# A two-layer hybrid trunk: gate rows kept as rows in a DRAM table and fetched by DMA, and a rotary step with one temporary

## The chip, the cores and the metric

One Trainium2 chip, one core. The metric is the device time of one execution in microseconds; an execution that is profiled gives a span (first to last instruction of the program) and its own device time beside it. The engines are TensorE (PE for matmuls, PEld for weight loads), VectorE (DVE), ScalarE (ACT), GpSimd (POOL) and SyncE (SP), which issues DMA transfers.

## The reference, cut to what matters

A trunk of two layers over 256 latent and 256 context tokens of width 1024, all in float32. Each layer is a half-step SwiGLU block, a mixing block (gated MLP over chunks, differential attention, windowed attention, joined by one output projection) and a second half-step SwiGLU block. Each block is modulated by nine vectors that come from a conditioning vector:

```python
def adaln_in(s, g_pre, shift, scale):
    return rmsnorm(s, g_pre) * (1 + scale) + shift

def adaln_out(s, y, g_post, gate, weight):
    return s + weight * gate * rmsnorm(y, g_post)

mod_x = (silu(c) @ w_mod[l] + b_mod[l]).reshape(b_, 9, 1, 1024)      # for latent tokens
mod_h = (silu(c_ctx) @ w_mod[l] + b_mod[l]).reshape(9, 1, 1024)      # for context tokens
# vectors 3j, 3j+1, 3j+2 are shift, scale and gate of block j (0: first FFN, 1: mixing, 2: second FFN)
# weight is 1/2 for the FFNs and 1 for the mixing

rot = jnp.concatenate([-x2, x1, -x4, x3], axis=-1)                   # quarters of a head
return x * cos + rot * sin                                           # apply_rope, latent q and k alone
```

In the last layer the context tokens take part only as keys and values.

## The kernel before, in words

Activations lie feature-major in Yh and Yl (128 partitions, 8 blocks of features, 512 tokens): a float32 number is split in a high part in the matmul's rounded format (hi, Yh, Uh) and the rest (lo, Yl, Ul), and a product is three matmuls, hi by hi, hi by lo and lo by hi (acc3, acc3_multi). Weights come in chunks of up to 1 MB into one of three staging buffers (tag stg), all issued by SyncE, and are split by ScalarE (L231) and VectorE or GpSimd (L100) into one of three pairs hi and lo.

A feed-forward block runs over pairs of 128-wide blocks of the 2816 hidden features, in three phases (6, 8 and 8 blocks); hidden() makes tanh, products and the split of a hidden block, in buffers of the tag p (six of them, function half). After each phase down() projects back. In the last phase the result of a token block is multiplied by the gate rows gp (L496), scaled by its norm and added to the stream S in residual(), and turn_y() normalises, transposes and modulates it for the next block. The mixing block makes keys, queries and values (L673 to L695 apply the rotary step to the latent ones), and then softmax units, spatial gating, normalisations and transposes are interleaved with the remaining projections.

The interleaving is by a model clock: every matmul helper calls tick() with its columns, and generators that are due (softmax units, turn_y, halves of the modulation) emit their next piece there; drain(tag) runs a kind of piece to its end. The order that the program text has is then used as priority by the framework's planner, which may move an instruction ahead in its engine's queue when its operands and its buffer allow it: a load of the second layer's mixing parameters (dl, L630) is issued at 544.61 us, in the middle of the first mixing. Buffers of one tag are reused in turn, and every queue, SyncE's and GpSimd's too, is in order.

The modulation is made by halves (mod_half, 512 of one vector's 1024 values): VectorE sums the eight 128-row slices of the weights, times the conditioning, into two accumulators of 128 partitions (L343, L345); four matmuls with ones add the partitions and spread each sum over 32 partitions (L350); ScalarE copies it (L355); two transposes turn it feature-major (L359), and mod_put adds the bias, multiplies by the norm's gain and writes coef (L322 to L331). 32 halves run so, two weight chunks each, about one in a step of the feed-forward loops; twelve of them are gates (q % 3 == 2). The first eight blocks' shift and scale come from mod_first.

gate_rows(l, j, st) makes two tiles gp of 128 x 512 in which every partition holds the gate row of a block for one kind of tokens: it is called once for each kind of tokens, twice in each of three feed-forward blocks and in the first mixing, once in the last mixing and in the last block: ten calls, each of 2 x 4 matmuls of a broadcast coefficient column with the identity (L401) and two ScalarE copies (L405).

## Time and profile before

| what | value |
|---|---|
| time, median of 3 runs | 1799.17 us (1795.40 to 1800.07) |
| the profiled execution: time, span | 1797.35 us, 1795.6 us |
| granted TensorE clock, mean over the span | 0.995 |
| busy: PE, PEld | 1749.6 us (97%), 1472.5 us (82%) |
| busy: DVE, ACT, POOL | 1188.4 us (66%), 709.9 us (40%), 161.1 us (9%) |
| moved by DMA | 250.79 MB, mean 140 GB/s |
| chain that ended last | PE 85%, DVE 7%, ACT 3%, POOL 2%, issue 2%, DMA 1% |

Busy time is the union of an engine's instructions. Matmuls are pipelined: a record of a 512-column matmul is about 0.37 to 0.39 us long, while the next one starts 0.23 us later, so the price of a matmul on its queue is read from the distance of starts. A small TensorE operation is listed twice where the float32 operand takes two passes.

### The profile page before, as it was taken

How to read it: one execution, taken by the hardware profiler on the slowest of the kernel's cores; microseconds unless marked ns; L12 is line 12 of the kernel's file. 1: busy time of each engine (PE TensorE's matmuls, PEld its weight loads, DVE VectorE, ACT ScalarE, POOL GpSimd, SP SyncE). 2: the span in 40 equal slices, each digit the busy share in tenths (PEclk: the TensorE clock that was granted, in tenths of full speed). 3: DMA queues.
4: the chain of work that ended last, by engine and by line, in shares of the span. 5: the costliest groups of instructions: out<-in, count | busy, mean ns of one | idle time of the engine just before them, and what ended most of it. 6: DMA issues, size and time to landing. Idle time of an engine off the chain costs nothing.

```text
span 1795.6 us, 24957 instructions
## 1 busy us (share of the span) xinstructions
PE 1749.6 (97%) x9847; PEld 1472.5 (82%) x9847; DVE 1188.4 (66%) x2195; ACT 709.9 (40%) x1520; POOL 161.1 (9%) x149
## 2 busy tenths in 40 slices
PE   6999999999999999999999999999999999999998
PEld 4788888889877689888787898787788897689997
DVE  4866876875467567668866476778764655765654
ACT  3323313244376653233222343332233535755443
POOL 3000000022312120000000120000000331010000
PEclk9999999999999999999999999999999999999999
DMA  9545554533120134465554233655544133226552
GB/s 327 192 135 182 188 188 141 164 124 106 59 95 27 35 96 153 138 202 165 180 171 141 70 100 121 203 169 195 174 142 141 46 96 118 71 89 194 188 188 71
DMA packets 190002, 250.79 MB, mean 140 GB/s; under 512 B 4666, under 2 KB 127804, under 8 KB 189884
## 3 DMA queue, kind: packets, MB, share of 16 engines
q1 hardware_dynamic: 189884, 249.19, 42.7%
q8 instruction: 77, 1.26, 0.3%
q14 instruction: 41, 0.34, 0.1%
HBM read 248.12 MB, written 1.05 MB: 139 GB/s over the span
## 4 chain that ended last, share of the span: by engine, by line
PE 85%; DVE 7%; ACT 3%; POOL 2%; issue 2%; DMA 1%; POOLq 0%; DVEq 0%; ACTq 0%
PE pa L241 26%; PE pa L245 13%; PE pb L254 6%; PE pb L260 6%; PE pb L262 6%; PE pa L254 5%; PE pa L262 5%; PE pa L260 5%; PE pb L241 3%; DVE lo L100 2%; PE pb L245 1%; PE pa L1208 1%; PE pc L350 1%; PE pa L770 1%; PE pc L791 1%
## 5 line engine op out<-in xcount | busy, mean ns | idle before, releaser
L100 DVE TENSOR_TENSOR lo<-stg,hi 128x512 fp32r<-128x512 f32 (+2 forms) x468 | 365.3, 820 | 189.9 <-ACT hi L231 114.3
L231 ACT ACTIVATE hi<-stg 128x512 fp32r<-128x512 f32 (+3 forms) x508 | 325.2, 701 | 321.1 <-PE pa L254 106.3
L241 PE MATMUL pa<-Yh,hi 128*128 128x512 f32 (+1 forms) x1168 | 417.2, 366 | 0.0
L241 PE MATMUL pa<-Yl,hi 128*128 128x512 f32 (+1 forms) x1168 | 414.4, 364 | 0.0
L345 DVE SCALAR_TENSOR_TENSOR acc<-stg,sT,acc 128x512 f32<-128x512 f32 x448 | 306.8, 746 | 4.3 <-DMA stg<-in_w_mod_dram 4.3
L245 PE MATMUL pa<-Yh,lo 128*128 128x512 f32 (+1 forms) x1168 | 258.6, 363 | 0.0
L241 PEld LDWEIGHTS pa<-Yh,hi 128*128 128x128 f32 x1168 | 220.4, 189 | 40.9 <-issue 7.8
L241 PEld LDWEIGHTS pa<-Yl,hi 128*128 128x128 f32 x1168 | 220.5, 189 | 34.5 <-issue 1.2
L245 PEld LDWEIGHTS pa<-Yh,lo 128*128 128x128 f32 x1168 | 202.2, 189 | 35.3 <-DVE lo L100 0.3
L543 ACT ACTIVATE Uh<-ha 128x512 fp32r<-128x512 f32 (+1 forms) x92 | 50.6, 551 | 278.7 <-DVE ha L541 278.7
L254 PE MATMUL pb<-hi,Ul 128*128 128x512 f32 x400 | 157.1, 393 | 0.0
L260 PE MATMUL pb<-hi,Uh 128*128 128x512 f32 x400 | 156.9, 393 | 0.0
L262 PE MATMUL pb<-lo,Uh 128*128 128x512 f32 x400 | 156.0, 390 | 0.0
L496 POOL TENSOR_TENSOR Z<-Z,gp 128x512 f32<-128x512 f32 x14 | 20.0, 1430 | 1179.5 <-ACT pb L495 1179.5
L541 DVE TENSOR_TENSOR ha<-ha,pa 128x512 f32<-128x512 f32 (+1 forms) x91 | 53.3, 585 | 82.5 <-PE pa L245 81.7
L260 PE MATMUL pa<-Yh,hi 128*128 128x256 f32 x368 | 92.0, 285 | 0.0
L262 PE MATMUL pa<-Yl,hi 128*128 128x256 f32 x368 | 91.3, 283 | 0.0
L539 ACT ACTIVATE ht<-pa 128x512 f32<-128x512 f32 (+1 forms) x91 | 46.5, 511 | 111.6 <-PE pa L245 82.8
L254 PEld LDWEIGHTS pb<-hi,Ul 128*128 128x128 f32 x400 | 75.1, 188 | 16.6 <-issue 1.2
L262 PEld LDWEIGHTS pb<-lo,Uh 128*128 128x128 f32 x400 | 75.1, 188 | 15.7 <-DVE lo L100 0.4
L260 PEld LDWEIGHTS pb<-hi,Uh 128*128 128x128 f32 x400 | 75.2, 188 | 15.5 <-issue 0.4
L100 POOL TENSOR_TENSOR lo<-stg,hi 128x512 fp32r<-128x512 f32 (+3 forms) x44 | 70.0, 1597 | 179.5 <-ACT hi L231 167.6
(290 smaller groups left out, 2772.1 us busy)
## 6 DMA issues: line engine op xcount, KB each, us to landing
stg<-in_w_mod_dram SPq DMA_DIRECT2D x64, 1024.0 KB, 5.1
stg<-in_ffn_w_gate_dram SPq DMA_DIRECT2D x43, 1024.0 KB, 5.4
stg<-in_ffn_w_up_dram SPq DMA_DIRECT2D x43, 1024.0 KB, 5.3
stg<-in_ffn_w_down_dram SPq DMA_DIRECT2D x32, 1024.0 KB, 5.0
stg<-in_w_in_dram SPq DMA_DIRECT2D x14, 1024.0 KB, 5.2
stg<-in_ffn_w_down_dram SPq DMA_DIRECT2D x16, 768.0 KB, 4.5
mst<-in_w_mod_dram SPq DMA_DIRECT2D x8, 1024.0 KB, 9.2
stg<-in_w_out_dram SPq DMA_DIRECT2D x8, 1024.0 KB, 6.2
```

What stands on the lines that cost most here:

```text
L100: eng.tensor_tensor(lo, full, f32(hi), op=ALU.subtract)
L231: nc.scalar.activation(hi[:, a:b, :], v[:, a:b, :], AF.Copy)
L241: nc.tensor.matmul(o, lhsT=ah, rhs=r, start=(i == 0), stop=(i == n - 1))
L245: nc.tensor.matmul(o, lhsT=al, rhs=bh, start=(i == 0), stop=(i == n - 1))
L254: nc.tensor.matmul(o, lhsT=al, rhs=bh, start=False, stop=last, skip_group_check=True)
L260: nc.tensor.matmul(o, lhsT=ah, rhs=bh, start=(first and k == 0), stop=False, skip_group_check=True)
L262: nc.tensor.matmul(o, lhsT=ah, rhs=bl, start=False, stop=False, skip_group_check=True)
L345: nc.vector.scalar_tensor_tensor(a, v[:, k, :], sc, a, op0=ALU.mult, op1=ALU.add)
L496: (nc.vector if hf else nc.gpsimd).tensor_tensor(zv, zv, gp[hf], op=ALU.mult)
L539: nc.scalar.activation(t, g, AF.Tanh, scale=0.5)
L541: nc.vector.tensor_tensor(a, a, u, op=ALU.mult)
L543: nc.scalar.activation(uh, a, AF.Copy)
```

## The change

The gate vectors no longer go through coef. A gate half keeps its sums as rows: the bias and the gain of the norm are loaded by SyncE, spread over the same 32-partition groups (by_groups, four transfers of 32 partitions x 256 values each), VectorE adds and multiplies in that layout, and GpSimd issues four stores of one partition's 256 values into a small table in DRAM (gtab). gate_rows becomes two fetches by SyncE, each of 512 values of a table row into all 128 partitions; in down() and in the first mixing it is called after the weights of the first half have been requested. norm_post is no longer in the parameter columns par. The transposes and mod_put of the other halves are put in a list (flips) which is emptied behind the next half's matmuls or when a modulation tag is drained. In the rotary step ScalarE writes the destination itself, which is then shuffled into the one temporary, multiplied in place by GpSimd and added to by VectorE.

```diff
@@ -75,6 +75,7 @@
     psc = ctx.enter_context(tc.tile_pool(name="psc", bufs=2, space=PSUM))
+    dr = ctx.enter_context(tc.tile_pool(name="dr", bufs=1, space=bass.MemoryType.DRAM))
     cnt = [0]
@@ -130,9 +131,17 @@
+    flips = []
+    def flip_now():
+        while flips:
+            flips.pop(0)()
     def drain(tag):
...
             run_next()
+        if tag[0] == "m":
+            flip_now()
@@ -152,7 +161,9 @@
     Yl = big.tile([P, KB, NT], F32R, name="Yl")
-    coef = const.tile([P, DEPTH, 9, KB, 2], F32, name="coef")
+    coef = const.tile([P, DEPTH, 3, 2, KB, 2], F32, name="coef")
+    gtab = {(l, j): dr.tile([2, D], F32, name=f"gate{l}{j}") for l in range(DEPTH) for j in range(3)}
@@ -162,17 +173,15 @@
     nc.sync.dma_start(rows[16:64, :], norm_pre.rearrange("l j (r p) -> (l j r) p", p=P))
-    nc.sync.dma_start(rows[64:112, :], norm_post.rearrange("l j (r p) -> (l j r) p", p=P))
-    nc.sync.dma_start(rows[112:114, :], diff_subln)
+    nc.sync.dma_start(rows[64:66, :], diff_subln)
     load_in(cx[0], 2)
-    par = const.tile([P, 114], F32, name="par")
+    par = const.tile([P, 66], F32, name="par")
     pt = pc()
-    nc.tensor.transpose(pt[:, 0:114], rows[0:114, :], ident[0:114, 0:114])
-    nc.vector.tensor_copy(par, pt[:, 0:114])
-    nc.vector.tensor_scalar(par[:, 16:112], par[:, 16:112], math.sqrt(D), None, op0=ALU.mult)
+    nc.tensor.transpose(pt[:, 0:66], rows[0:66, :], ident[0:66, 0:66])
+    nc.vector.tensor_copy(par, pt[:, 0:66])
+    nc.vector.tensor_scalar(par[:, 16:64], par[:, 16:64], math.sqrt(D), None, op0=ALU.mult)
     npre = par[:, 16:64].rearrange("p (l j b) -> p l j b", l=DEPTH, j=3)
-    npost = par[:, 64:112].rearrange("p (l j b) -> p l j b", l=DEPTH, j=3)
@@ -311,8 +320,8 @@
     def mod_put(l, q, b, n, src, mid):
-        dst = coef[:, l, q, b:b + n, :]
         j, kind = q // 3, q % 3
+        dst = coef[:, l, j, kind, b:b + n, :]
@@ -322,13 +331,16 @@
         nc.vector.tensor_tensor(mid, src, bias, op=ALU.add)
-        if kind == 1:
-            nc.vector.scalar_tensor_tensor(dst, mid, 1.0, bc(npre[:, l, j, b:b + n]),
-                                           op0=ALU.add, op1=ALU.mult)
-        else:
-            nc.vector.scalar_tensor_tensor(dst, mid, 1.0 if j == 1 else 0.5,
-                                           bc(npost[:, l, j, b:b + n]), op0=ALU.mult,
-                                           op1=ALU.mult)
+        nc.vector.scalar_tensor_tensor(dst, mid, 1.0, bc(npre[:, l, j, b:b + n]),
+                                       op0=ALU.add, op1=ALU.mult)
+    def by_groups(src):
+        r = wk.tile([P, 256], F32, tag="sq", name=nm("gr"), bufs=7)
+        for j in range(4):
+            nc.sync.dma_start(r[32 * j:32 * j + 32, :],
+                              src[256 * (j % 2):256 * (j % 2) + 256].partition_broadcast(32))
+        return r
@@ -344,24 +356,43 @@
                                                        op1=ALU.add)
+        gate = q % 3 == 2
+        j = q // 3
+        if gate:
+            br = by_groups(b_mod[l, c0:c0 + 512])
+            gr = by_groups(norm_post[l, j, hf * 512:(hf + 1) * 512])
         yield T_MOD
         t = pc()
-        for j in range(4):
-            nc.tensor.matmul(t[32 * j:32 * j + 32, 0:256], lhsT=ones[:, 0:32],
-                             rhs=acc[j // 2][:, 256 * (j % 2):256 * (j % 2) + 256],
-                             start=True, stop=True, tile_position=(0, 32 * j))
+        for i in range(4):
+            nc.tensor.matmul(t[32 * i:32 * i + 32, 0:256], lhsT=ones[:, 0:32],
+                             rhs=acc[i // 2][:, 256 * (i % 2):256 * (i % 2) + 256],
+                             start=True, stop=True, tile_position=(0, 32 * i))
         tick(1024)
+        flip_now()
+        if gate:
+            w = math.sqrt(D) * (1.0 if j == 1 else 0.5)
+            nc.vector.tensor_tensor(br, t[:, 0:256], br, op=ALU.add)
+            nc.vector.scalar_tensor_tensor(br, br, w, gr, op0=ALU.mult, op1=ALU.mult)
+            for i in range(4):
+                f0 = hf * 512 + 256 * (i % 2)
+                nc.gpsimd.dma_start(gtab[l, j][i // 2:i // 2 + 1, f0:f0 + 256],
+                                    br[32 * i:32 * i + 1, :])
+            return
         ev = wk.tile([P, 256], F32, tag="sq", name=nm("modev"), bufs=7)
         nc.scalar.activation(ev, t[:, 0:256], AF.Copy)
-        yield T_FLIP
-        u = pc()
-        for i in range(2):
-            nc.tensor.transpose(u[:, i * P:(i + 1) * P], ev[:, i * P:(i + 1) * P], ident)
-        tick(600)
-        uv = u[:, 0:256].rearrange("p (i s h r) -> p h i s r", i=2, s=2, h=2)
-        tmp = sm.tile([P, 2, 2, 2], F32, tag="modt", name=nm("modt"))
-        for h in range(2):
-            mod_put(l, q, 4 * hf + 2 * h, 2, uv[:, h, :, :, 0], tmp[:, h])
+        def turn():
+            u = pc()
+            for i in range(2):
+                nc.tensor.transpose(u[:, i * P:(i + 1) * P], ev[:, i * P:(i + 1) * P], ident)
+            tick(600)
+            uv = u[:, 0:256].rearrange("p (i s h r) -> p h i s r", i=2, s=2, h=2)
+            tmp = sm.tile([P, 2, 2, 2], F32, tag="modt", name=nm("modt"))
+            for h in range(2):
+                mod_put(l, q, 4 * hf + 2 * h, 2, uv[:, h, :, :, 0], tmp[:, h])
+        flips.append(turn)
@@ -396,13 +427,7 @@
         for hf in range(2):
-            t = pc()
-            for i in range(4):
-                nc.tensor.matmul(t[:, i * P:(i + 1) * P],
-                                 lhsT=coef[:, l, 3 * j + 2, 4 * hf + i, st:st + 1].to_broadcast([P, P]),
-                                 rhs=ident, start=True, stop=True)
-            tick(1600)
-            nc.scalar.activation(gp[hf], t, AF.Copy)
+            nc.sync.dma_start(gp[hf], gtab[l, j][st, hf * 512:(hf + 1) * 512].partition_broadcast(P))
         return gp
@@ -439,8 +464,8 @@
                     nc.scalar.activation(f[:, i * n:(i + 1) * n], t[:, i * n:(i + 1) * n], AF.Identity,
-                                         scale=coef[:, l, 3 * j + 1, b0 + i, st:st + 1],
-                                         bias=coef[:, l, 3 * j, b0 + i, st:st + 1])
+                                         scale=coef[:, l, j, 1, b0 + i, st:st + 1],
+                                         bias=coef[:, l, j, 0, b0 + i, st:st + 1])
                 fv = f.rearrange("p (b q) -> p b q", b=nb)
@@ -485,7 +510,7 @@
             st = sidx(s)
-            gp = gate_rows(l, j, st)
+            gp = []
             ss = {tb: sm.tile([P, 2], F32, tag="ss", name=nm("ss")) for tb in own}
@@ -509,6 +534,8 @@
                     ws[hf] = [chunk(hf, 0), chunk(hf, 1, into)]
+                if not hf:
+                    gp[:] = gate_rows(l, j, st)
                 for tb in own:
@@ -638,7 +665,7 @@
         gs = const.tile([P, 1], F32, name=nm("gsub"))
-        nc.vector.tensor_scalar(gs, par[:, 112 + l:113 + l], 1.0 - lam_init, None, op0=ALU.mult)
+        nc.vector.tensor_scalar(gs, par[:, 64 + l:65 + l], 1.0 - lam_init, None, op0=ALU.mult)
         sk = const.tile([P, 4], F32, name=nm("sink"))
@@ -670,14 +697,14 @@
         def rope_evac(dst, ps, scale):
-            scr = wk.tile([P, 256], F32, tag="t256", name=nm("scr"))
-            nc.scalar.activation(scr, ps, AF.Copy, scale=scale)
+            nc.scalar.activation(dst, ps, AF.Copy, scale=scale)
             sh = wk.tile([P, 256], F32, tag="t256", name=nm("shf"))
-            nc.vector.stream_shuffle(sh, scr, shmask)
-            nc.gpsimd.tensor_tensor(scr, scr, ropet[:, 0, :], op=ALU.mult)
+            nc.vector.stream_shuffle(sh, dst, shmask)
             nc.vector.tensor_tensor(sh, sh, ropet[:, 1, :], op=ALU.mult)
-            nc.vector.tensor_tensor(dst, sh, scr, op=ALU.add)
+            nc.gpsimd.tensor_tensor(dst, dst, ropet[:, 0, :], op=ALU.mult)
+            nc.vector.tensor_tensor(dst, dst, sh, op=ALU.add)
@@ -1114,7 +1141,7 @@
             st = sidx(s)
-            gp = gate_rows(l, 1, st)
+            gp = []
             bank = pb if s == HS else pa
@@ -1131,6 +1158,8 @@
                     ws[1][1] = chunk(1, 1)
+                if hf == hfs[0]:
+                    gp[:] = gate_rows(l, 1, st)
                 for tb in tbs[s]:
@@ -1175,7 +1204,7 @@
                     t = XT[:, b, s[0]:s[1]]
-                    nc.vector.tensor_scalar(t, t, coef[:, 0, 1, b, i:i + 1], coef[:, 0, 0, b, i:i + 1],
+                    nc.vector.tensor_scalar(t, t, coef[:, 0, 0, 1, b, i:i + 1], coef[:, 0, 0, 0, b, i:i + 1],
                                             op0=ALU.mult, op1=ALU.add)
...
                     nc.scalar.activation(yh, t, AF.Copy)
```

## Rows read from the trace of the kernel before

**Rows 1.** Sums by stage: start:end, length; PE, PEld, DVE, ACT, POOL busy; clock; DMA.
```profile
60.00:425.00 365.00, 365.00 (x1730) 295.88 (x1729) 272.63 (x458) 123.07 (x223) 17.30 (x15) 1.00 0.50 162
...
452.00:685.00 233.00, 220.45 (x1448) 185.95 (x1447) 150.33 (x358) 132.29 (x375) 51.76 (x42) 0.99 0.22 74
685.00:1435.00 750.00, 749.32 (x3797) 623.59 (x3797) 511.11 (x863) 244.82 (x453) 33.32 (x31) 1.00 0.45 146
1435.00:1605.00 170.00, 158.98 (x1099) 137.59 (x1098) 109.31 (x238) 93.71 (x237) 33.19 (x30) 0.99 0.29 94
1605.00:1795.60 190.60, 183.38 (x1288) 172.32 (x1286) 107.28 (x181) 85.30 (x161) 4.31 (x4) 0.98 0.48 155
```

**Rows 2.** Groups by line, whole span: shapes xcount | busy us, mean ns | idle before.
```profile
L401 PE MATMUL pc<-ident,coef 128*128 128x128 f32 x160 | 20.0, 275 | 0.8 <-ACT CU L797 0.8
L359 PE MATMUL pc<-ident,modev 128*128 128x128 f32 x64 | 12.2, 271 | 0.0
L880 DVE TENSOR_TENSOR gq<-gq,gx 128x256 f32<-128x256 f32 x12 | 5.1, 423 | 0.2
L324 DVE TENSOR_TENSOR modt<-pc,bm 128x4 f32<-128x4 f32 x44 | 5.0, 154 | 3.0 <-PE pc L359 3.0
```

**Rows 3.** Timeline of weight loads before the first block's last projection: start us, us.
```profile
362.05 0.37 PEld L359 LDWEIGHTS pc<-ident,modev 128*128 128x128 f32 x2
362.39 0.19 PEld L241 LDWEIGHTS pa<-Yh,hi 128*128 128x128 f32 x1
...
365.05 1.98 PEld L401 LDWEIGHTS pc<-ident,coef 128*128 128x128 f32 x16
366.94 0.19 PEld L260 LDWEIGHTS pb<-hi,Uh 128*128 128x128 f32 x1
```

**Rows 4.** Timeline of matmuls of two calls of gate_rows in the first mixing.
```profile
588.30 1.16 PE L401 MATMUL pc<-ident,coef 128*128 128x128 f32 x8 [0.79 <-ACT CU L797]
...
639.89 1.95 PE L401 MATMUL pc<-ident,coef 128*128 128x128 f32 x16
```

**Rows 5.** DMA issues by line: xcount, KB each, median us from issue to landing.
```profile
stg<-in_w_mod_dram SPq DMA_DIRECT2D x64, 1024.0 KB, 5.1
...
bs<-in_gmlp_b_s_dram SPq DMA_DIRECT2D x8, 32.0 KB, 3.3
```

**Rows 6.** Timeline of SyncE's queue: start us, us, xcount issues in a row.
```profile
53.70 1.83 SPq L650 DMA_DIRECT2D bs<-in_gmlp_b_s_dram  x3
```

**Rows 7.** Waits, whole span: who waited for whom: us in total, times, longest us.
```profile
SPq L203 <- DVE lo L100: 1018.6, 138, 44.7
...
ACT hi L231 <- PE pa L254: 106.3, 16, 12.7
...
ACT hi L231 <- PE pa L241: 80.2, 39, 3.1
```

**Rows 8.** Timeline of TensorE: the matmuls of two gate halves of the first block.
```profile
246.21 0.64 PE L350 MATMUL pc<-acc,ones 128*32 128x256 f32 x8
...
269.04 0.64 PE L350 MATMUL pc<-acc,ones 128*32 128x256 f32 x8
```

**Rows 9.** Timeline, last weights of the first block's last projection: split, first use.
```profile
379.94 1.72 DVE L100 TENSOR_TENSOR Yl<-stg,Yh 128x1024 fp32r<-128x1024 f32 x1
...
382.26 0.39 PE L260 MATMUL pb<-Yh,Uh 128*128 128x512 f32 x1
```

**Rows 10.** Timelines of ACT and PE at both mixings' rotary steps; [idle before <- releaser].
```profile
474.53 0.38 ACT L675 ACTIVATE scr<-pa 128x256 f32<-128x256 f32 x1 [2.01 <-DVE QK L680]
474.81 0.76 ACT L948 ACTIVATE VG<-pb 128x320 f32<-128x320 f32 x2
475.30 0.41 PE L241 MATMUL pb<-hi,Yh 128*128 128x320 f32 x1 [2.42 <-ACT VG L948]
...
1442.63 0.38 ACT L675 ACTIVATE scr<-pa 128x256 f32<-128x256 f32 x1 [4.22 <-DVE QK L680]
...
1443.98 0.44 PE L436 MATMUL pb<-ident,Z 128*128 128x128 f32 x2 [2.54 <-ACT yf L441]
```

## Prediction

> **What bounds the kernel now.** I read the sums by stage first. The two feed-forward blocks of layer 0 and the first of layer 1 lie in the stretches 60 to 425 and 685 to 1435 us, the last one behind 1605; the two mixings lie in 452 to 685 and 1435 to 1605. In the feed-forward stretches TensorE is busy 365.0 of 365.0 and 749.3 of 750 us at a granted clock of 1.00, the upper of its two levels, while VectorE, the next, has 75% and 68% [rows 1]. There every instruction taken off TensorE's queue should move the end by its own issue time, as long as nothing else is just behind. In the mixings it stands idle for 12.6 of 233 and 11.0 of 170 us [rows 1]: TensorE is still the first limit, but in places it waits for an answer from ScalarE, and work removed beside such a wait is worth nothing. The table of groups by line gives the removed work its size [rows 2], the timeline of the weight loads what one removal is worth on the queue [rows 3].
>
> **Gate rows without matmuls.** There are ten calls of gate_rows, 160 matmul records in all, 20.0 us busy [rows 2], two records to each of 80 matmuls. On the queue, the weight loads of one call begin at 365.05 and those of the next work at 366.94 [rows 3]: 1.89 us. Seven calls lie in feed-forward blocks (two each in three, one in the last): 7 x 1.89 = 13.2 us. Three lie in mixings. In one the second half waited 0.79 us more for a PSUM bank [rows 4], so it could give 2.7 us; the other two ran through, as at 639.89 [rows 4], for up to 1.9 each. The bounds are 0 and 6.5; TensorE is idle only about 6% there, so most of a removal should count, but the softmax units that interleave have chains of their own. I take 2.9. The ScalarE copies that go with them cost nothing now and give nothing: ScalarE is busy a third of a feed-forward stretch [rows 1].
>
> **Gate halves without transposes.** Twelve of the 32 halves of the modulation are gates. Each loses two transposes: 362.05 to 362.39 on the queue [rows 3], 0.34 us, times 12 is 4.1 us, all in feed-forward stretches. The other 20 keep theirs and only run them behind the next half's matmuls: the same work later, and its readers are drained for. One is left over into the first mixing and keeps one of seven buffers of the tag sq until the drain. I give that nothing.
>
> VectorE loses four small operations in a gate half (154 ns for such a one) and gets two of 128x256. The nearest row is 423 ns for that size [rows 2]: 0.85 for 0.62 us, 0.2 us more, 2.8 us in all on an engine with a quarter of the stretch free. Nothing; if the cover were gone, 2.8 us.
>
> **The new transfers.** In each gate half SyncE issues eight loads of 32 KB, 96 in all, and GpSimd four stores, 48 in all; SyncE issues 20 fetches of a 2 KB row into 128 partitions, 256 KB. Loads of 32 KB that are spread in the same way land in 3.3 us [rows 5], and three of them took SyncE 1.83 us to issue [rows 6], 0.61 each. So 96 x 0.61 = 58.6 us of SyncE's time is new, 4.9 us a gate half, and it stands ahead of weight loads. What hides it: SyncE stood 1018.6 us before weight loads until a staging buffer was split, and the splits in turn stood 186.5 us, in 55 waits, 3.4 us each, until TensorE had read an older copy [rows 7]. With a weight so early that its split waits for TensorE, and two more chunks of copies ahead of it, 4.9 us once in 23 us, the distance of two halves [rows 8], are covered. I take nothing; the upper end is the second rival.
>
> The stores have no row in this trace, as nothing is issued from GpSimd. Below, nothing; above, GpSimd's share of the splits and the power of the norms would stand behind a waiting store. GpSimd is busy 17.3 of 365 us and 33.3 of 750 [rows 1], and the last gate half of the first block has its matmuls at 269 us [rows 8], a hundred before the last down projection, so nothing urgent queues behind. If each cost the 0.61 us of a load's issue it would be 29 us of an idle engine. I take nothing. The round trip through DRAM isn't late either: the table of that half is read in the mixing at 588 [rows 4]. The fetch waits for its two buffers of the tag p, which the copies needed at the same place of the ring; it is 20 x 0.61 = 12 us of SyncE's time, and the weights of the down projection's second half are behind it. In the first block that is tight: their last part was split at 381.66 and first read at 382.26 [rows 9], and TensorE would now come 1.9 us sooner. Up to 1.9 us can be lost there.
>
> A page speaks against all this. The Trainium skill, "DMA: Bandwidth & Descriptors", section "Rules for kernel authors", asks for many small transfers to be merged into a large one, since below 64 KB mostly overhead is paid, and the page's fit has about 2.0 us fixed for each. By that, as an estimate, 96 loads one behind the other are some 200 us, and the change would lose. The trace agrees that a small one is dear in latency (3.3 us for 32 KB against 5.1 for 1 MB [rows 5]), but three were issued within 1.83 us [rows 6], so they don't wait for each other's landing.
>
> **The rotary step.** Before, ScalarE writes a temporary, and two temporaries of one step fill the ring of two, so each step waits for the last addition of the one before. At 1442.63 ScalarE had stood 4.22 us for it, the scaled copies for the next tokens queued behind it, and TensorE stood 2.54 us until 1443.98. In the first mixing the same wait, 2.01 us, held the copy of V until 474.81, and TensorE stood 2.42 us until 475.30 [rows 10]. Now ScalarE writes the destination and waits for nothing of the step. Both stalls should go: 5.0 us. GpSimd's multiply comes in the same place, and VectorE has the same three operations. Bounds: a gain of 7 if the units behind also start earlier, a loss of 2 if the copies run ahead and the same engines' splits of the next weights come later instead. I take 4.0.
>
> At the start one transfer leaves SyncE's queue, at most 0.6 us [rows 6]; I take nothing.
>
> **Sum.** 13.2 + 4.1 + 2.9 + 4.0 = 24.2 us. The profiled execution took 1797.35 us (span 1795.6 and 1.75 around it), so 1773.2. It lies 1.8 us below the median of the runs shown, 1799.17, against which the forecast is 1799.17 - 24.2, about 1775 us. With the bounds of the terms, from 17.3 + 0 - 2 to 17.3 + 6.5 + 7, it is 1768 to 1784.
>
> **The rivals.** First, only the feed-forward part reaches the end: the mixings have other chains (norm, softmax, turn) and give back what they gain, or lose 2 us, and the tight spot of [rows 9] takes 1.9. That leaves 12 to 16 us: 1783 to 1787. For it speaks that VectorE and ScalarE are each over half busy there [rows 1]; against it, that the two stalls of [rows 10] have a cause which is gone.
>
> Second, on the other side: SyncE's queue gets late. The place is a gate half, 4.9 us of small issues ahead of the next weight load. If there were no cover, 58.6 us are lost against 24.2 gained: 1799 + 34, about 1833 us. It decides from 24.2 / 12 = 2.0 us of late weights for each gate half. For it: SyncE's queue is in order, and VectorE, which splits and also sums the halves, is busy three quarters of the time [rows 1], so a late weight isn't made up quickly. Against it: the 186.5 us in which splits waited for TensorE [rows 7]. The rule of the skill would make it likely; the rows don't.
>
> Third, the same cause by half: 1.6 to 2.5 us of each gate half are late (19 to 30 us in all), and the time stays within 0.3%, 1794 to 1805 us. About 0.3% is what a measurement of this kernel can tell from no change.
>
> **How the numbers follow.** The forecast has 0.68, the first rival 0.17, the second 0.08, the third 0.07. The forecast and the first rival are both faster by over 0.3%: 0.85; the same 0.07, slower 0.08. The forecast's own range is 1768 to 1784; with the first rival and some room for what the order of the queues does, 1767 to 1790 holds eight in ten.
>
> **What would show it.** Right: no matmul in gate_rows, 20 fetches in its place; TensorE still busy all of the feed-forward stretches, each shorter by 1.89 us for a call and 0.34 for a gate half; ScalarE's copies of the rotary step without a wait, and no stall of 2.5 us at the turn of the second mixing and at the first copies of V. Wrong: splits that wait for weight loads where they waited for TensorE, gaps on TensorE after gate halves, a fetch that SyncE holds for long with weights behind it, or GpSimd's stores under a wait with a norm behind them.

## The result and the profile after

The changed kernel takes 1767.63 us, the median of four runs (1765.01 to 1769.63), against 1798.2 us (four runs) of the kernel before on the same chip: a ratio of 0.9831, 95% interval 0.9814 to 0.9847, so 27 to 33 us faster. The forecast was 1775 us, 24 us faster, with a range from 1767 to 1790. The side was right; the gain was undersized by about 6 us. The time lies 0.4 us below the forecast's own 1768 to 1784 and 0.6 us inside the stated range, which is less than single executions differ by. The profiled execution took 1767.02 us, its span is 1765.1 us.

The page of the kernel after begins with busy times (share of the span) and instructions of each engine:

```profile
PE 1723.8 (98%) x9663; PEld 1450.0 (82%) x9663; DVE 1190.5 (67%) x2171; ACT 694.6 (39%) x1488; POOL 184.1 (10%) x197
```

Sums by stage of the kernel after, in the stretches of [rows 1] but for the last, which ends earlier; same columns:

```profile
60.00:425.00 365.00, 363.55 (x1732) 295.91 (x1731) 274.07 (x451) 123.52 (x226) 26.07 (x32) 1.00 0.52 171
...
452.00:685.00 233.00, 225.66 (x1513) 191.66 (x1512) 159.56 (x382) 134.24 (x379) 44.91 (x39) 1.00 0.25 83
685.00:1435.00 750.00, 747.59 (x3788) 623.42 (x3788) 521.52 (x869) 244.21 (x451) 59.91 (x74) 1.00 0.47 153
1435.00:1605.00 170.00, 161.11 (x1103) 139.41 (x1102) 102.29 (x220) 94.84 (x241) 22.44 (x19) 0.99 0.30 100
1605.00:1765.00 160.00, 152.46 (x1032) 141.04 (x1030) 90.93 (x150) 69.62 (x128) 4.00 (x4) 0.99 0.52 168
```

TensorE is still the bound. But its idle time in the feed-forward stretches has grown from 0.0 and 0.7 us to 1.5 and 2.4 us: something is late there that was not late before. In the first mixing it has shrunk from 12.6 to 7.3 us, and in the second from 11.0 to 8.9. The stretches stand at the same clock times while the work moved by some 30 us, so a second reading is needed.

Both kernels have the same 8328 matmuls on split operands. I took the start of the k-th one in each trace and subtracted. The table says how far the kernel after is ahead (medians of 13 neighbours; the time is that of the kernel before):

```
before, us   ahead, us   what lies between
    49          2.7      start
   320          4.4      8 non-gate and 4 gate halves (first block)
   395          6.7      2 gate_rows calls
   480         12.1      first mixing: turn, rotary step
   571         13.2
   644         17.9      2 gate_rows calls in the first mixing
   958         19.4      8 non-gate and 2 gate halves (second block)
  1032         23.2      2 gate_rows calls
  1063         21.1      the turn of the last stream: given back
  1359         23.1      4 non-gate and 6 gate halves (third block)
  1403         26.7      2 gate_rows calls
  1445         29.0      second mixing: rotary step
  1541         33.8      another order of the work, no gain
  1615         29.4      the order is the same again; 1 gate_rows call between
  1777         30.8      last gate_rows call
```

Such a table holds where both kernels have started the same other work by then. Between 1500 and 1590 us, and between 585 and 640, they haven't: at 1541 the kernel after has, beside the removed ones, twelve records fewer of the softmax units' small matmuls and transposes behind it than the kernel before, and at 1590 as many. So 33.8 is work put off, and the step from 29.0 to 29.4 is what counts.

Now the rows that answer to the forecast's signs. Groups by line of the kernel after; gate_rows has no group on TensorE any more, and GpSimd has 48 stores:

```profile
L388 PE MATMUL pc<-ident,modev 128*128 128x128 f32 x40 | 8.6, 296 | 0.0
...
L379 POOL DMA_DIRECT2D gate<-gr x48 | 24.0, 507 | 573.9 <-DVE gr L376 573.9
```

From 64 transposes 40 are left [rows 2]. The loads, by line (min/median/max ns to issue, first and last start):

```profile
L341 SPq DMA_DIRECT2D gr<-in_b_mod_dram x48: 311/420/577, 48.8 to 1269.6; - x48
...
DMA to landing us min/median/max: 1.7/4.1/6.1
```

A load of 32 KB takes SyncE 0.42 us, not the 0.61 that I took from [rows 6], and lands in 4.1 us. The gains' 48 loads have a median of 0.42 us too. The 96 take 40 us. Waits over the whole span of the kernel after:

```profile
SPq L212 <- DVE lo L101: 919.0, 136, 42.0
...
SPq L430 <- PE pa L781: 24.5, 1, 24.5
...
ACT hi L240 <- PE pa L263: 100.3, 15, 12.5
...
ACT hi L240 <- PE pa L250: 75.0, 38, 3.1
```

SyncE's wait for splits fell by 99.6 us from 1018.6 [rows 7], and the 40 us of loads have room in that. The splits still stand 175.3 us until TensorE has read an older copy (186.5 before). One fetch held SyncE for 24.5 us, until 603.9 us in the first mixing, and no engine waits for a weight from then until 667 us.

At the rotary steps ScalarE's row of [rows 10] with its wait for VectorE's addition has no counterpart; its copies now wait for TensorE alone (timeline of ScalarE after, both mixings):

```profile
472.07 0.44 ACT L975 ACTIVATE VG<-pb 128x320 f32<-128x320 f32 x1 [3.08 <-PE pb L254]
...
1423.52 0.66 ACT L702 ACTIVATE QK<-pa 128x256 f32<-128x256 f32 x2 [4.97 <-PE pa L263]
```

### The profile page after: what moved, and what is told of

It is laid out like the page before. It is cut to its first block, busy times and chain, and to the rows that moved or that the text cites. A ratio compares the mean times of both kernels' runs of the same rounds, so it can differ in the third digit from the quotient of the medians.

```text
span 1765.1 us, 24835 instructions
## 1 busy us (share of the span) xinstructions
PE 1723.8 (98%) x9663; PEld 1450.0 (82%) x9663; DVE 1190.5 (67%) x2171; ACT 694.6 (39%) x1488; POOL 184.1 (10%) x197
## 5 line engine op out<-in xcount | busy, mean ns | idle before, releaser
L101 DVE TENSOR_TENSOR lo<-stg,hi 128x512 fp32r<-128x512 f32 (+2 forms) x468 | 360.1, 808 | 193.4 <-ACT hi L240 123.6
L379 POOL DMA_DIRECT2D gate<-gr x48 | 24.0, 507 | 573.9 <-DVE gr L376 573.9
```

Of the source, the lines that this page charges most:

```text
L101: eng.tensor_tensor(lo, full, f32(hi), op=ALU.subtract)
L379: nc.gpsimd.dma_start(gtab[l, j][i // 2:i // 2 + 1, f0:f0 + 256], br[32 * i:32 * i + 1, :])
```

## The experiments

Each kernel is compared with the kernel before on the same chip; where two variants of the kernel after are compared with each other, their intervals against before are mostly too wide to part them, and I say which lines of the traces decide.

**The rotary step alone, and the gates alone.** Kernel before with the new step:

```diff
-            scr = wk.tile([P, 256], F32, tag="t256", name=nm("scr"))
-            nc.scalar.activation(scr, ps, AF.Copy, scale=scale)
+            nc.scalar.activation(dst, ps, AF.Copy, scale=scale)
...
-            nc.vector.stream_shuffle(sh, scr, shmask)
-            nc.gpsimd.tensor_tensor(scr, scr, ropet[:, 0, :], op=ALU.mult)
+            nc.vector.stream_shuffle(sh, dst, shmask)
...
-            nc.vector.tensor_tensor(dst, sh, scr, op=ALU.add)
+            nc.gpsimd.tensor_tensor(dst, dst, ropet[:, 0, :], op=ALU.mult)
+            nc.vector.tensor_tensor(dst, dst, sh, op=ALU.add)
```

> The kernel before with the new rotary step alone. Theory: the gain of the rotary step is its own, two stalls of TensorE behind ScalarE's wait for the ring of temporaries (2.4 us at the first copies of V, 2.5 us at the second mixing's turn) and the short gaps around them: 5 to 8 us faster than before, ratio 0.9955 to 0.997, and no wait of ScalarE's scaled copy for the last addition. Rival: the time that the whole change won in the first mixing (TensorE's matmuls stood 6.7 us earlier at 395 us of before and 17.9 us earlier at 644 us) comes from the gate part, so the step alone gives under 3 us, ratio over 0.998.

Measured: 1788.72 us against 1796.69, ratio 0.9957 (0.9944 to 0.997): 8 us faster, 5.4 to 10.1 by the interval. The forecast's term was 4.0. In the table's terms its trace gains 6.7 us in the first mixing (395 to 571) and 2.8 at 1445.

The other half is the kernel after with the same diff reversed.

> The changed kernel with the old rotary step. Theory: the parts add up, so it keeps 23 to 26 of the 30.6 us, ratio 0.9855 to 0.987. Rival: the parts need each other in the mixings, and it keeps under 20 us, ratio over 0.989.

Measured: 1778.19 us, ratio 0.9899 (0.9886 to 0.9913): 18.2 us faster, 15.6 to 20.5. That is below the 23 to 26 of the theory and inside the rival. The terms that the forecast had for this part, 13.2 + 4.1 + 2.9 = 20.2 us, lie inside the interval; it is the rest of the 30.6 us, the rotary step, that was taken too small. The two ratios together make 25.9 us (21.0 to 30.6), the whole change 30.4 (27.5 to 33.4). The intervals overlap, so that the halves help each other, the rival's reason, is not shown.

**What in the rotary step.** Kernel before, old step, but its first temporary from the ring of seven:

```diff
-            scr = wk.tile([P, 256], F32, tag="t256", name=nm("scr"))
+            scr = wk.tile([P, 256], F32, tag="sq", name=nm("scr"), bufs=7)
```

> The kernel before with the old rotary step of two temporaries, one of which comes from the ring of seven (tag sq) instead of the ring of two. Theory: what the rotary step wins is the wait of ScalarE for the ring, not the one temporary: the same 5 to 8 us as the new step alone. Rival: it is that ScalarE writes the destination (one buffer less to be passed on, another order on VectorE and GpSimd), then this gives under 2 us.

Measured: 1792.19 us, ratio 0.9975 (0.9965 to 0.9986): 4.5 us, 2.5 to 6.3. In the kernel before ScalarE's waits at this line were (whole span):

```profile
ACT scr L675 <- DVE QK L680: 34.3, 14, 5.7
```

With the larger ring that group is gone, and what is left at the line are waits for TensorE, the longest of them

```profile
ACT scr L675 <- PE pa L254: 8.4, 4, 5.0
```

So the ring's wait was real, and its removal by itself is worth about half of what the new step brings, between the theory and the rival. The two intervals overlap a little, but on this chip each run of the new step (1787.53 to 1790.47 us) is faster than each run with the larger ring (1790.83 to 1794.14). Of the difference the traces show 1.3 us, between 482 and 571 us, where the softmax units begin; the rest I did not separate.

**The start.** Kernel before with the load of the bias table moved behind the first weights of the modulation:

```diff
-    load_bm(0)
-
...
+    load_bm(0)
```

> The kernel before with the bias load moved behind the first two w_mod loads, so that seven transfers stand before the first w_mod load instead of eight; the parameter columns stay at 114. Theory: the ninth transfer of SyncE waits for the landing of the first (5.78 us in before, 3.58 after), so this gives the 2.7 us by which the changed kernel is ahead at 60 us: w_mod's first load issued at about 3.2 us instead of 5.8, 2 to 3 us faster, ratio 0.9985. Rival: the gain at the start comes from the shorter parameter load and transpose, then under 0.6 us.

Measured: 1797.42 us, ratio 1.0005 (0.9995 to 1.0015): at most 0.9 us faster. In its trace it was 1.5 us ahead at 49 us. The kernel after is 2.7 us ahead there, and the eight other kernels that share its start, 1.3 to 4.2 us; but of the three others whose start is that of the kernel before (rotary step alone, larger ring, and the next one), two are 2.0 us ahead as well and one is 1.8 behind. So the theory's 2 to 3 us did not show, though the first w_mod load was issued at 3.59 us as in the kernel after. A lead of some 2 us may be there, and what executions differ by is as large.

**The transposes held back, alone.** Kernel before, with the 32 halves' transposes collected and run behind the next half's matmuls, and everything else as it was:

```diff
-        yield T_FLIP
-        u = pc()
-        for i in range(2):
-            nc.tensor.transpose(u[:, i * P:(i + 1) * P], ev[:, i * P:(i + 1) * P], ident)
...
+        def turn():
+            u = pc()
+            for i in range(2):
+                nc.tensor.transpose(u[:, i * P:(i + 1) * P], ev[:, i * P:(i + 1) * P], ident)
...
+        flips.append(turn)
```

> The kernel before, with all 24 pairs of transposes of the modulation halves held back until the next half's matmuls, and nothing else of the change. Theory (the transposes of a half, issued right behind the half's four matmuls, save TensorE a separate weight change and a gap, which is seen in the kernel after as about 0.1 us at each non-gate half): 24 halves by 0.1 us is 2.4 us, so 1.5 to 4 us faster, a ratio of 0.998 to 0.9995. Rival (the steps of 0.1 us come from matmuls that shift for other reasons, and the saving is the eight gate halves' transposes alone, which this kernel keeps): within 1 us of the kernel before. A second rival: holding the halves' results back makes somebody wait, 2 us or more slower.

(The expectation speaks of 24 halves; there are 32.) Measured: 1794.87 us, ratio 0.9984 (0.9974 to 0.9994): 2.9 us faster, 1.1 to 4.7. By the ledger, the table above taken for this kernel, the three blocks' halves gave 1.0, 1.0 and 1.1 us in the table's stretches, 3.2 in 32 halves, 0.10 each. The whole change gave 1.7, 1.5 and 2.0 there, 5.2. So the moved transposes are worth 0.1 us a half though TensorE's work stays, and that twelve pairs go away altogether a further 2.0.

**Is SyncE's queue covered?** Kernel after, with every small load cut in two (192 loads), and in four (384):

```diff
-            nc.sync.dma_start(r[32 * j:32 * j + 32, :],
-                              src[256 * (j % 2):256 * (j % 2) + 256].partition_broadcast(32))
+            for p0 in range(32 * j, 32 * j + 32, 16):
+                nc.sync.dma_start(r[p0:p0 + 16, :],
+                                  src[256 * (j % 2):256 * (j % 2) + 256].partition_broadcast(16))
```

The second has 8 in place of 16.

> The kernel after, with each load of a gate half's bias and norm rows cut in two (16 partitions each instead of 32): 192 loads instead of 96, about 40 us more of SyncE's issue time, 3.4 us more per gate half. Theory (SyncE's queue runs so far ahead of its consumers that the loads' issue time lies under it): within 0.3% of the kernel after, 1762 to 1773 us. Rival (the small loads push the weight loads behind them, the prediction's second rival): each gate half ends 1 us or more later where its loads stand, 15 us or more slower in all, 1783 us or above.

> The kernel after, with each load of a gate half's bias and norm rows cut in four (8 partitions each): 384 loads instead of 96, so that a gate half has 32 loads at some 0.42 us of SyncE, 13.4 us instead of 3.4, about 120 us more of SyncE's time in the whole program. Theory (a load of a half still lies under the waits of SyncE's queue for VectorE's weight splits, as the run with 192 loads showed no cost): within 0.3% of the kernel after, 1762 to 1773 us, or at most 5 us slower where two gate halves follow one another. Rival (from some number of loads on SyncE's queue is the bound; the prediction put the point at 2.0 us per half): 10 us each for the eight halves that are not covered, up to 80 us, 1790 us or above.

Measured: 1767.08 us, ratio 0.9826 (0.981 to 0.9842), and 1766.29 us, ratio 0.9822 (0.9805 to 0.9839). Neither can be told from the kernel after. The issue time and SyncE's wait with 192 loads:

```profile
L342 SPq DMA_DIRECT2D gr<-in_b_mod_dram x96: 310/418/1549, 47.4 to 1279.4; - x96
```

```profile
SPq L212 <- DVE lo L101: 891.4, 136, 42.0
```

and with 384:

```profile
L342 SPq DMA_DIRECT2D gr<-in_b_mod_dram x192: 271/293/1042, 47.4 to 1297.5; - x192
```

```profile
SPq L212 <- DVE lo L101: 857.4, 130, 42.0
...
ACT hi L240 <- DMA stg<-in_ffn_w_gate_dram: 49.6, 12, 20.6
```

SyncE issued 192 x 0.42 = 80 us and 384 x 0.29 = 113 us of small loads, and its wait for splits shrank instead. With 384 a weight was late for a split by 20.6 us once (8.1 us the longest in the kernel after), and that too cost nothing that shows: the copies ahead lasted. A half had 32 loads, about 9.4 us, and no lateness of 2.0 us a half, the rival's point, reached TensorE.

**Where the feed-forward gain went.** Two places in the ledger: the turn at 1063 us, and the first block's calls, 2.3 us instead of 3.8. At the first, TensorE's timeline of the kernel after:

```profile
1035.72 0.27 PE L461 MATMUL pb<-ident,Z 128*128 128x128 f32 x1
1037.41 0.98 PE L461 MATMUL pb<-ident,Z 128*128 128x128 f32 x7 [1.42 <-DVE Z L447]
...
1040.55 0.66 PE L461 MATMUL pb<-ident,Z 128*128 128x128 f32 x4 [0.72 <-ACT yf L466]
```

VectorE normalises the rows that TensorE turns. Here are VectorE in the kernel after, VectorE in the kernel before, and TensorE in the kernel before:

```profile
1036.87 0.88 DVE L447 TENSOR_SCALAR Z<-S,r 128x512 f32<-128x512 f32 x2 [0.44 <-POOL r L424]
```

```profile
1058.01 0.88 DVE L422 TENSOR_SCALAR Z<-S,r 128x512 f32<-128x512 f32 x2 [0.44 <-POOL r L393]
```

```profile
1058.55 1.04 PE L436 MATMUL pb<-ident,Z 128*128 128x128 f32 x8
```

TensorE comes 22.8 us sooner (1035.72 for 1058.55), but the rows that it turns are normalised only 21.1 us sooner (1036.87 for 1058.01). The kernel after with the turn planned later:

```diff
-PACE_IN1, PACE_OUT1, PACE_DRAIN1, T_CHAIN, T_LATE = 1.5, 1.2, 1.2, 7.5, 10.5
+PACE_IN1, PACE_OUT1, PACE_DRAIN1, T_CHAIN, T_LATE = 1.5, 1.2, 1.2, 7.5, 13.0
```

> The kernel after, with the planner's time for the turn of the last stream of a block moved from 10.5 to 13.0 us behind, so that TensorE has more other work before it asks for the normalised rows. Theory (2.1 us that the gate rows gained by 1032 us are given back at 1035 us, where the turn now waits 1.69 us for VectorE's normalised rows, and a part of this at 366 and 1425 us): the wait shrinks, 1.5 to 4 us faster than the kernel after, some 1763.5 to 1766 us. Rival (VectorE's chain is late whatever TensorE does first, and the wait moves to the next block's first projection): within 1 us of the kernel after, or up to 3 us slower.

Measured: 1764.36 us (1763.74 to 1766.56), ratio 0.9814 (0.9797 to 0.983). The interval overlaps that of the kernel after. But on the same chip a kernel that differs from the kernel after in nothing that its trace shows (the smaller distance between halves below, 1766.94 to 1768.59) has no run as fast as the slowest of these four, and the place shows it:

```profile
1036.21 1.03 PE L461 MATMUL pb<-ident,Z 128*128 128x128 f32 x8
...
1039.61 0.66 PE L461 MATMUL pb<-ident,Z 128*128 128x128 f32 x4 [0.94 <-ACT yf L466]
```

The wait of 1.42 us is gone, the one behind it has grown from 0.72 to 0.94. In the ledger this kernel gains 1.4 us on the kernel after there.

At the second place VectorE and TensorE of the kernel after look so:

```profile
357.47 4.72 DVE L357 SCALAR_TENSOR_TENSOR acc<-stg,sT,acc 128x512 f32<-128x512 f32 x7
...
364.63 3.40 DVE L357 SCALAR_TENSOR_TENSOR acc<-stg,sT,acc 128x512 f32<-128x512 f32 x5
...
368.22 1.22 DVE L101 TENSOR_TENSOR lo<-stg,hi 128x1024 fp32r<-128x1024 f32 x1
```

```profile
367.51 1.20 PE L367 MATMUL pc<-acc,ones 128*32 128x256 f32 x8 [0.55 <-DVE acc L357]
369.49 0.50 PE L271 MATMUL pb<-lo,Uh 128*128 128x512 f32 x1 [0.78 <-DVE lo L101]
```

The last half's sums fill VectorE, and the split of the projection's next weights stands behind them; TensorE waits for both. In the kernel before it has no wait between 352 and 400 us. The first try to move that half was a smaller distance between halves:

```diff
-T_MOD, T_FLIP, MOD_PACE = 15.0, 2.5, 18.0
+T_MOD, T_FLIP, MOD_PACE = 15.0, 2.5, 14.0
```

> The kernel after, with the planner's distance between two modulation halves cut from 18 to 14 us, so that the last half of the first block (its 16 sums on VectorE at 357 to 368 us) comes some 12 us earlier and no longer meets the last down projection's eviction. Theory (of the 3.8 us that the two gate calls of the first block should have given, 1.6 were lost there to VectorE): 1 to 2 us faster than the kernel after. Rival (the weights of a half, 4 MB of w_mod in all per quarter, then come too early for their buffers, and TensorE waits for halves elsewhere): no gain, or up to 5 us slower.

Measured: 1767.54 us, ratio 0.983 (0.9814 to 0.9846). It tested nothing: the half didn't move, its sums stand at 357.64 us in that trace. The kernel asks for halves only between pairs of columns, and at these places 18 us had already gone by. The direct test takes VectorE's work away:

```diff
-            for k in range(4):
+            for k in range(1 if (l, q, hf) in ((0, 7, 0), (0, 7, 1)) else 4):
```

> The kernel after, with the sums of the last two modulation halves of the first block cut from 16 instructions to 4 each (the products of three of every four rows of these halves are left out, so the shift of the first mixing stage is wrong), which takes 24 of VectorE's 0.65 us instructions off the stretch in front of 368 us. Theory (the first block's two gate calls gave 2.2 us instead of the 3.8 of the two in the second because VectorE is busy without a gap from 357 to 368 us and its weight split comes late): TensorE's gaps of 0.9 and 1.2 us at 366 and 368 us go, 1 to 2 us faster than the kernel after. Rival (VectorE would be late anyway, for the evictions of the last projection): no difference at 395 us beyond 0.3 us.

(These halves are of vector 7, so what the kernel leaves out is in the scale of the second feed-forward block, not in the shift of the first mixing.)

Measured: 1764.42 us (1762.88 to 1766.06), ratio 0.9813 (0.9795 to 0.983). The stretch in the kernel after and in this one (columns as in [rows 1]):

```profile
360.00:375.00 15.00, 13.67 (x65) 10.29 (x64) 14.37 (x23) 6.75 (x10) 0.19 (x1) 1.00 0.77 254
```

```profile
360.00:375.00 15.00, 15.00 (x67) 12.39 (x66) 6.97 (x12) 5.99 (x9) 2.73 (x2) 1.00 0.73 254
```

VectorE falls from 14.37 to 6.97 us, TensorE has no gap, and its lead over the kernel after grows by 3.1 us at 375 us, 2.3 of which are left at 389: the theory held. That is more than the 1.5 us that were missing; the kernel before had these sums as well, without a wait of TensorE.

**A version that keeps what was given back.** Late turn, and two halves of the first block asked for earlier:

```diff
                 step()
+                if first and pi == 1 and fp in (0, 4):
+                    step(1)
```

> The kernel after, with two changes that go with what the runs showed: the turn of a block's last stream at 13.0 instead of 10.5 us (as in the run with the late turn, 3 us faster than the kernel after), and two modulation halves of the first block asked for earlier (one more step behind the first and the third pair of columns of its second phase), so that no half is summed while the last down projection starts at 360 us. Theory: the late turn's 3 us and 1 to 2 us of the tight spot at 366 us together, 1762 to 1764 us. Rival (the earlier halves take VectorE and the weights' buffers where TensorE needs the next weights): 1765 us or above, with new gaps between 200 and 300 us.

Measured: 1773.21 us, ratio 0.9862 (0.9845 to 0.9879): slower than the kernel after, as the rival had it. The early halves made TensorE stand twice (timeline of TensorE, then of VectorE, in front of it):

```profile
233.95 1.08 PE L367 MATMUL pc<-acc,ones 128*32 128x256 f32 x8 [3.90 <-DVE coef L334]
...
237.93 0.79 PE L271 MATMUL pb<-lo,Uh 128*128 128x512 f32 x1 [2.89 <-DVE lo L101]
238.52 0.63 PE L263 MATMUL pb<-hi,Ul 128*128 128x512 f32 x1
238.94 0.63 PE L271 MATMUL pb<-lo,Uh 128*128 128x512 f32 x1
```

```profile
214.78 6.05 DVE L357 SCALAR_TENSOR_TENSOR acc<-stg,sT,acc 128x512 f32<-128x512 f32 x9
...
224.31 9.36 DVE L357 SCALAR_TENSOR_TENSOR acc<-stg,sT,acc 128x512 f32<-128x512 f32 x14
```

Against the late turn alone the ledger has 10.7 us lost between 203 and 235 us, and 2.1 regained at 374, about what the short sums gave. It is VectorE again: the sums of one half directly behind those of another, and TensorE's matmul of the half first in its queue. The two waits are 6.8 us of the 10.7. Behind them the clock is low: it reads 0.50 from 233.2 to 243.2 us, and the matmuls from 238.52 to 243.21 start 0.43 us apart instead of 0.23, another 2.2 us. The last run asks for one half, in the middle of a pair of columns:

```diff
                         hidden(g[:, 0:n], u[:, 0:n], fp + i, full)
+                        if first and pi == 1 and fp == 4 and not i:
+                            step(1)
                 step()
```

> The kernel after, with the turn of a block's last stream at 13.0 instead of 10.5 us, and one modulation half of the first block asked for earlier (an extra step in the middle of the third pair of columns of the second phase, so not together with another half as in the run before), so that the last half is summed some 20 us before the last down projection. Theory: 3 us of the late turn and the 2 us that the shortened sums gave at 366 us, together 1761 to 1763 us. Rival (a half put between two others makes TensorE wait for its sums, as it did for 4.3 and 3.5 us in the run before): above 1764 us, with a new gap between 235 and 290 us.

Measured: 1763.81 us (1762.62 to 1764.3, five runs), ratio 0.9816 (0.9803 to 0.9829). Every run lies below the lowest of the kernel after, 1765.01, though the kernel before was 2 us lower on this chip too (1796.08). From 360 to 375 us TensorE is busy all 15.00 us. The time lies between the theory and the rival. Of the 2.1 us that it gains on the late turn alone at 374 us it had lost 1.8 between 46 and 231, so it can't be told apart from the late turn alone.

## Why the prediction was right, and where its sizes were off

**The bound and the side: right.** TensorE's queue sets the end of the feed-forward stretches, and most of what was taken off it there came out at the end.

**Gate rows in the feed-forward blocks, 13.2 us: the calls gave 11.1** (2.3, 3.9, 3.5 and 1.4 for two, two, two and one), and 2.1 went back at the turn, so 9.0 net. The two calls of the second block gave 3.9 against 3.8 forecast, so 1.9 us a call is the right price of the queue's time; why the single call of the last block gave 1.4 I did not look into. What failed is "as long as nothing else is just behind": in two places VectorE was just behind. I had expected the loss in the first block at the fetch and the weights behind it [rows 9]; it was there, and of that size, but from the sums of a half. The short sums show this. Of the rival that the feed-forward part alone reaches the end, only this giving back was true. (Its own terms make 13.4 to 15.4 us, not 12 to 16.)

**Gate halves' transposes, 4.1 us: 5.2.** Here two errors partly cancel. The term that I put at nothing, the 20 that are only moved, was not nothing: holding back all 32 gave 2.9 us, 0.1 each, so these are 2.0 of the 5.2. That leaves 3.2 for the twelve that are gone, 0.26 each and not 0.34. I didn't read that a pair in the middle of other matmuls costs more than beside the next half's. Which part of the 0.1 us is a weight load and which a gap was not measured.

**The two mixings, 2.9 + 4.0 = 6.9 us: about 14**, and these are the terms that were sized wrong. By the ledger the first mixing went from 6.7 to 17.9 us ahead, 11.2, and the second from 26.7 to 29.4, 2.7.

The gate rows were discounted without need in the first mixing. Its two calls gave 4.7 us (571 to 644), all of the 2.7 + 1.9 that the queue's time comes to; the softmax units' own chains took nothing of it, and at most 0.5 us of the 4.7 is the clock (below). In the second mixing the discount was right: the call there gave 0.4 (1445 to 1615).

The rotary step gave the rest: 6.5 us in the first mixing and 2.7 in the second. In the second that is the stall of [rows 10], 2.54 us. In the first the ledger rises in four steps. The stall of 2.42 us gives 2.6 at 474 us. In front of it, at 468, are 1.3 us that I had not read: TensorE stood twice for splits of the weights, whose high parts were behind the rotary copies in ScalarE's queue. In the kernel before:

```profile
466.76 0.41 PE L241 MATMUL pb<-lo,Yh 128*128 128x320 f32 x1 [0.31 <-POOL lo L100]
467.78 0.42 PE L241 MATMUL pb<-lo,Yh 128*128 128x320 f32 x1 [0.46 <-DVE lo L100]
```

The run with the larger ring gains the same 1.3 and 2.6 us there, so both are ScalarE's wait. Behind the stall come 1.6 us, at 482, which are the clock, and by 565 another 1.1, in the softmax units, which I did not take apart.

The clock reads so in the kernel before (columns as in [rows 1], the clock is third from the end):

```profile
476.50:479.90 3.40, 3.40 (x15) 3.40 (x14) 0.41 (x1) 0.00 (x0) 0.00 (x0) 0.50 0.00 0
602.80:606.20 3.40, 3.40 (x13) 1.90 (x11) 1.91 (x9) 1.21 (x5) 1.01 (x1) 0.50 0.00 0
1602.90:1606.20 3.30, 2.79 (x13) 2.80 (x14) 2.41 (x5) 0.00 (x0) 0.00 (x0) 0.50 0.02 6
```

0.50 is the lower of the two levels, 1.2 GHz; the first stretch begins 1.2 us after the stall that ended at 475.30. What it costs can be read from two kernels that have the same stall of 2.4 us and no low clock behind it, the gates alone and the transposes held back:

```profile
473.00:481.00 8.00, 8.00 (x54) 6.95 (x52) 2.36 (x7) 1.67 (x6) 0.00 (x0) 1.00 0.01 2
```

```profile
473.00:481.00 8.00, 8.00 (x55) 7.47 (x54) 1.18 (x3) 1.22 (x3) 0.24 (x1) 1.00 0.01 2
```

Both gain 1.5 us on the kernel before between 474 and 482 us; the kernel with the bias load moved, which has the low clock there (473.9 to 477.3), gains nothing. So whether these 1.5 us are lost depends on the execution: the low clock followed the same stall in two of four traces, and it stands there in none of the ten traces without the stall. The stretch at 602.80 cost next to nothing: the three traces that lack it and have the work of the kernel before there (larger ring, bias load, transposes held back) are 0.5 us better to 0.5 us worse over 571 to 644. In the second mixing the kernel after has one stretch, as the kernel before has:

```profile
1575.20:1578.50 3.30, 3.30 (x17) 3.30 (x17) 0.44 (x2) 1.27 (x4) 0.00 (x0) 0.50 0.61 201
```

So the rotary step without the clock is about 7.7 us, close to the 8.0 (5.4 to 10.1) that it measured alone, against 4.0: it had been valued at its two stalls of 5.0 us with a fifth taken off.

That the whole lies inside the range is in part luck: the gate rows in the feed-forward blocks were taken 4 us too large and the mixings 7 too small, and a run 0.7 us faster at the median would have left it.

**Transfers at nothing: right.** The second and third rivals fall: with four times as many loads nothing shows. The price was also smaller, 0.42 us a load instead of 0.61. The Trainium skill, "DMA: Bandwidth & Descriptors", section "Rules for kernel authors", which speaks against loads under 64 KB, holds here for the latency of one (4.1 us for 32 KB) and not for the kernel's time; the 2.0 us for each, from which the prediction made 200 us, are that page's fit for transfers that GpSimd issues, and these were SyncE's. The same table's advice to issue early and wait late is what this kernel does, and the 384 loads agree with it. GpSimd's stores had no row before: 484 ns to issue, 1.7 us to land at the median; the next other work in GpSimd's queue starts 30 us or more behind them.

**The start at nothing:** the traces leave it between nothing and some 2 us; the order of the loads is at most 0.9 of it, by the run with the bias load moved. What else the shorter parameter load gives was not tested.

## What to carry to other kernels

Work taken off a bounding engine's in-order queue is worth its issue time only up to the next operand that another engine brings: list, for each place, which split, sum or normalised row arrives next and by how much it was early, and move that work too. Small loads from a queue that itself waits for buffers are free as long as that wait is longer than their issue time; read the queue's own waits, not the transfers' sizes. A stall of TensorE can cost its waiting time and a stretch of low clock behind it, which another execution of the same work may not have; look at the granted clock after each stall, and in more than one trace, before you price it. A table of k-th starts finds the places at once, but read it only where both kernels have started the same other work.

## What the runs showed of the hardware

- The granted clock falls to 0.50 for short stretches inside a program that TensorE fills by 97 to 98%. Between the first 32 us and the end, and beside the one at 233 us above, the fourteen traces have them at five places only, told in the time of the kernel before: 476 us (2 traces), 603 (2), 1444 (2), 1533 (6) and 1604 (12). In the kernel before a wait of TensorE of 1.5 to 2.5 us stands at or just in front of each (475.30, 601.42, 1443.98, 1532.05 and 1603.41 us), but only three of the five had the low clock; the kernel with 384 loads had none. They cost by the ledger 1.5 us at 476, 3.1 at 1533, where they are about twice as long as elsewhere, some 1.3 at 1604 and 0.5 or less at 603.
- With this, much of the spread between executions of one kernel is clock. Of 19 runs of the kernel before on the chip of the first experiments the two with a mean clock of 0.992 took 1802.6 us, the eight with 0.996 took 1795.7 us on average.
- Two transposes cost about 0.1 us less beside four other short matmuls than alone between long ones, in 32 places, with TensorE's work unchanged and VectorE's few operations behind them moved along (2.9 us, 1.1 to 4.7).
- An issue of a small load takes SyncE less time when there are more, smaller ones: 0.42 us for 32 partitions and for 16, 0.29 us for 8.
